# Last products of an encoder layer's MLP: row halves one after the other, the last product by output rows, and a shorter inverse root

## The chip, the cores and the metric

The kernel runs on one core of a Trainium2 chip. The metric is the device time of one execution in microseconds (us). The kernel before took 3382.24 us, the median of three runs (3379.86 to 3386.33).

## The reference

One layer of an encoder on 2048 rows of 1024 numbers, all in fp32, and a last RMSNorm:

```python
u = _rms_norm(h, norm_mix_g[l])
proj = u @ w_in[l]
hy = _short_conv_centred(proj[..., :HY_COLS], hy_conv_w[l], hy_conv_b[l])
spec = _hyena_filter_spectrum(L, hy_filt_w1[l], ...)
y_hy = _group_rms_norm(_hyena(hy, spec, hy_skip[l]), hy_norm_g[l], HYENA_GROUPS)
...
y_ml = _group_rms_norm(_mlstm_bidirectional(...), ml_norm_g[l], MLSTM_HEADS)
mixed = jnp.concatenate([y_hy, y_ml], axis=-1)
h = h + mixed @ w_out[l]
h = h + _cross_attention(_rms_norm(h, norm_x_g[l]), _rms_norm(mem, norm_mem_g[l]), ...)
h = h + jnp.square(jax.nn.relu(_rms_norm(h, norm_ff_g[l]) @ ff_w1[l])) @ ff_w2[l]
return _rms_norm(h, final_norm_g)
```

`_rms_norm(x, g)` is `x * rsqrt(mean(x*x) + EPS) * g` over a row. The change touches the last product (`@ ff_w2`), the residual sum behind it, the last RMSNorm, and the inverse root of every norm.

## The kernel before, in words

**Stages.** Row norms, the input projection, the filters and the FFT convolution, the mLSTM, the output projection, cross-attention, and the MLP follow each other. Every fp32 operand of a large product is split into a high and a low half in a rounded format (`halves`, `split`): ACT casts the high half, and DVE or GpSimd (POOL) subtracts to get the low half. One product is then three matmuls (`mm3`, L294 to L297: high by high, low by high, high by low) that add up in one PSUM bank.

**The MLP.** Both of its products use a Strassen-Winograd scheme of seven products instead of eight. The last one, "down", runs over four quarters `o` of the inner dimension (4096), each with the seven products `i` in the order `ORDER_DOWN` = 1, 6, 7, 5, 3, 2, 4: 28 products `prods`, numbered n = 0 to 27. Each is done for two halves of the rows, `tp` = 0 and 1, and each such (n, tp) has four inner blocks k. So `down` lists 224 steps s = (n, tp, k); a step issues twelve matmuls of 128x512 (four output blocks m of 128, three matmuls each), a group (n, tp) 48. A group has four PSUM banks, of tag "mm" for half 0 and "hy" for half 1 (four buffers each). In the last block o = 3 (n = 21 to 27) the finished sums leave.

**Around a step.** `fetch_b(s + 3)` loads a block of activations `wr` from the scratch `hc` (DMA on SP's queue) and makes its halves `bh`, `bl` (six buffers each); from s = 200 on the subtraction is POOL's for k > 0. `fetch_a` makes the next product's weight halves `ah`, `al` (four buffers). Behind the last inner block four evictions add the banks into `acc[i, tp]` (L1576, DVE); the sums between the accumulators (`add`, L1542) run on DVE or POOL.

**The way out.** `acc` holds columns by rows; the output wants rows by columns. The list `outs` holds closures that are taken one or two at a time behind the steps' matmuls. `turn` (L1509 to L1512) makes four transposes of 128x128 on TensorE into a PSUM bank of the tag that the running group doesn't use, squares the bank on ACT with a sum per row into `ss` (L1511), and multiplies by the gain `gl` on DVE into another accumulator's space (L1512). `finish(c, ...)` (L1517 to L1533), for c = 0 to 3, 512 rows each, combines the two sums of squares with `rbp`, the earlier norm's 1/(mean square + EPS), takes the inverse root, scales eight tiles of 128x512 (ACT L1529, for the last row block DVE L1527 as well), and stores (L1533, SP's queue). Row blocks 1 and 3 finish earlier; block 0 finishes behind (27, 0) and block 2 behind (27, 1), the last group. The remaining turns and the finish of block 2 come after the loop (`for x in outs`).

**The inverse root.** `rsqrt` (L150 to L155) starts from a guess made on the number's bits, a shift and then a multiply and add, and does three Newton steps of three DVE instructions each. It is called 58 times, with names `xr`, `mr`, `hr`, `qr` and `or`.

**Order.** The instructions are ordered by a planner that estimates times (`schedule_with_timeline_sim=True`); the order in the text is only its starting point, except where `keep_in_program_order` pins an instruction. Pools with a fixed number of buffers set how far ahead it can go.

Of the kernel before, what the change touches and what calls it, by code (L numbers as in the profile page):

```python
# [19 lines left out]
D = 1024  # L20
# [77 lines left out]
class Prog:  # L98
# [45 lines left out]
    def rsqrt(self, pool, ms, name):  # L144
# [5 lines left out]
        nc.vector.tensor_scalar(yi, mi, 1, None, ALU.logical_shift_right)  # L150
        nc.vector.tensor_scalar(yi, yi, -1.0, float(0x5F3759DF), ALU.mult, ALU.add)
# [141 lines left out]
    def mm3(self, ps, lh, ll, rh, rl, start, stop):  # L293
        mm = self.nc.tensor.matmul  # L294
        mm(ps, lh, rh, start=start, stop=False)  # L295
        mm(ps, lh, rl, start=False, stop=False)  # L296
        mm(ps, ll, rh, start=False, stop=stop)  # L297
# [763 lines left out]
    def attention(self, es):  # L1061
# [66 lines left out]
        for c in range(4):  # L1128
# [134 lines left out]
            def stats(c=c, ssum=ssum):  # L1263
# [12 lines left out]
                nc.vector.reciprocal(rbp[:, 4 * c:4 * c + 4], rbp[:, 4 * c:4 * c + 4])  # L1276
# [12 lines left out]
    def halves(self, src, tags, bufs, eng):  # L1289
        hi, lo = (self.R.tile([128, 512], F32R, tag=n, name=n, bufs=bufs) for n in tags)  # L1290
        self.nc.scalar.copy(hi, src)  # L1291
        eng.tensor_tensor(lo, src, hi.bitcast(F32), ALU.subtract)  # L1292
        return hi, lo
# [72 lines left out]
    def ffn(self):  # L1366
# [7 lines left out]
        down = [(n, tp, k) for n in range(len(prods)) for tp in range(2) for k in range(4)]  # L1374
        aq, bq = {}, {}

        def fetch_a(n, k):
# [13 lines left out]
            aq[n, k] = self.halves(src, ("ah", "al"), 4, eng)  # L1391
# [90 lines left out]
        with tc.tile_pool(name="down", bufs=1) as B:  # L1482
# [21 lines left out]
            ss = B.tile([128, 4, 2, 4], F32, name="ss")  # L1504

            def turn(c, h, src, dst, t, tag):
# [5 lines left out]
                nc.vector.tensor_tensor(dst[:, t], pt, gl[:, 512 * h:512 * h + 512], ALU.mult)  # L1512

            def finish(c, dst, last):
                rb = self.rbp[:, 4 * c:4 * c + 4]
                m = B.tile([128, 4], F32, tag="mo", name="mo", bufs=2)
                nc.vector.tensor_tensor(m, ss[:, c, 0], ss[:, c, 1], ALU.add)  # L1517
                nc.vector.tensor_tensor(m, m, rb, ALU.mult)
                nc.vector.tensor_tensor(m, m, rb, ALU.mult)
                nc.vector.tensor_scalar(m, m, 1.0 / D, EPS, ALU.mult, ALU.add)  # L1520
                rv = self.rsqrt(B, m, "or")
                nc.vector.tensor_tensor(rv, rv, rb, ALU.mult)
                for h in range(2):
                    for t in range(4):
                        v = dst[h][:, t]
                        if last and t % 2:
                            nc.vector.tensor_scalar(v, v, rv[:, t:t + 1], None, ALU.mult)  # L1527
                        else:
                            nc.scalar.mul(v, v, rv[:, t:t + 1])  # L1529
                        if last and t % 2 or t == 3:  # L1530
                            n = 2 if last else 4
                            r0 = 512 * c + 128 * (t + 1 - n)
                            nc.sync.dma_start(  # L1533
                                out=self.out[r0:r0 + 128 * n, 512 * h:512 * h + 512].rearrange("(t p) c -> p t c", p=128),
                                in_=dst[h][:, t + 1 - n:t + 1])
# [3 lines left out]

            def add(i, j, tp, eng):  # L1540
                for m in range(4):
                    eng.tensor_tensor(acc[i, tp][:, m], acc[i, tp][:, m], acc[j, tp][:, m], ALU.add)  # L1542
# [3 lines left out]
            V, G = nc.vector, nc.gpsimd  # L1546
            for s, (n, tp, k) in enumerate(down):
# [3 lines left out]
                if s + 3 < len(down):  # L1551
                    fetch_b(s + 3, G if s > 199 and k else V)
# [6 lines left out]
                if k == 0:  # L1559
                    bank = [self.hy() if tp else self.mm() for _ in range(4)]  # L1560
                (ah, al), (bh, bl) = aq[n, k], bq.pop(s)
                for m in range(4):
                    msl = slice(128 * m, 128 * m + 128)
# [138 lines left out]
```

## Time and profile before

| | |
|---|---|
| median of three runs | 3382.24 us (3379.86 to 3386.33) |
| profiled execution, its own time | 3383.48 us |
| its span on the core | 3381.8 us |
| mean granted TensorE clock | 0.979 |
| TensorE busy (PE) | 3194.3 us, 94% |
| VectorE busy (DVE) | 2042.5 us, 60% |
| ScalarE busy (ACT) | 1492.4 us, 44% |
| GpSimd busy (POOL) | 1269.8 us, 38% |
| DMA | 674.55 MB, 199 GB/s over the span |

The durations come from the one profiled execution, and times in it count from the start of its span. A line of the timeline has start, duration, engine, line of the kernel, operation, and out<-in by the program's names; "xN" are N instructions taken together; what stands in brackets is the idle time of the engine just ahead and what ended it. A line of stretches gives the busy time of PE, PEld (weight loads), DVE, ACT and POOL, each with the number of instructions, then the granted clock, the DMA engines' share, and GB/s.

### The profile page before, as it was taken

Reading aid. Unit: us, or ns where it says so; the run is one execution under the profiler, and the core shown is the slowest. Engines: PE = TensorE matmul, PEld = TensorE weight load, DVE = VectorE, ACT = ScalarE, POOL = GpSimd, SP = SyncE. Lnnn points to the kernel's source line nnn. Section 1 sums busy time; section 2 is a strip of 40 time slices with the busy share of each in tenths; the row PEclk is TensorE's granted clock in tenths of the full one; section 3 lists DMA queues with packets and bytes.
Section 4 is the critical chain, followed back from the end, with each engine's and each line's share of the span. In section 5 each row is a group of like instructions: output and inputs, shape, how many; then the busy total and the mean of one; then the engine's idle time right before and its main releaser. Section 6 shows DMA issues by size and latency. Waiting matters only on the chain.

```text
span 3381.8 us, 46860 instructions
## 1 busy us (share of the span) xinstructions
PE 3194.3 (94%) x15671; PEld 2550.0 (75%) x15671; DVE 2042.5 (60%) x3711; ACT 1492.4 (44%) x2884; POOL 1269.8 (38%) x894
## 2 busy tenths in 40 slices
PE   6999999999898888799999999999999999999997
PEld 5646666677676788688887997788788887888876
DVE  7685225524546755777766554755855576555695
ACT  4344435523454235444444444555655543333335
POOL 2131001200222314544424012876766564434482
PEclk9999999999999999999999999999999999999998
DMA  5366889996998579857657444765654475444434
GB/s 165 117 208 206 286 282 256 271 325 238 241 240 279 172 229 273 275 154 231 184 162 253 147 132 161 224 205 179 207 167 158 147 244 171 128 140 135 133 94 159
DMA packets 480749, 674.55 MB, mean 199 GB/s; under 512 B 41738, under 2 KB 256848, under 8 KB 479484
## 3 DMA queue, kind: packets, MB, share of 16 engines
q1 hardware_dynamic: 478904, 668.70, 63.4%
q0 software_dynamic: 1600, 2.86, 0.4%
q8 instruction: 124, 2.03, 0.3%
q14 instruction: 117, 0.96, 0.1%
q10 hardware_dynamic: 4, 0.00, 0.0%
HBM read 452.23 MB, written 219.18 MB: 199 GB/s over the span
## 4 chain that ended last, share of the span: by engine, by line
PE 43%; DVE 7%; DMA 5%; issue 3%; POOL 2%; ACT 1%; SPq 1%; DVEq 0%; ACTq 0%; POOLq 0%
PE mm L295 9%; PE mm L297 9%; PE mm L296 9%; PE hy L297 5%; PE hy L295 4%; PE hy L296 4%; DVE wl L301 1%; DVE bl L1292 1%; POOL acc L1500 1%; DMA rw<-rows 1%; PE hy L1106 1%; DMA wr<-xs 1%; DMA wn<-in_x_dram 1%; DMA va<-vd 1%; DVE acc L1542 0%
## 5 line engine op out<-in xcount | busy, mean ns | idle before, releaser
L301 DVE TENSOR_TENSOR wl<-wn,wh 128x512 fp32r<-128x512 f32 (+1 forms) x352 | 274.6, 813 | 144.4 <-ACT wh L300 143.8
L1292 DVE TENSOR_TENSOR bl<-wr,bh 128x512 fp32r<-128x512 f32 x213 | 234.8, 1108 | 134.6 <-ACT bh L1291 132.2
L1291 ACT CAST ah<-w 128x512 fp32r<-128x512 f32 x284 | 176.2, 622 | 298.9 <-PE hy L296 152.7
L300 ACT CAST wh<-wn 128x512 fp32r<-128x512 f32 (+1 forms) x352 | 202.1, 617 | 216.2 <-PE mm L296 80.0
L295 PE MATMUL mm<-xh,wh 128*128 128x512 f32 x640 | 276.4, 432 | 8.7 <-ACT P L542 7.5
L739 POOL TENSOR_TENSOR b<-b,a 128x512 f32<-128x512 f32 x64 | 88.8, 1387 | 502.1 <-ACT b L737 201.1
L296 PE MATMUL mm<-xl,wh 128*128 128x512 f32 x640 | 266.4, 416 | 0.1
L297 PE MATMUL mm<-xh,wl 128*128 128x512 f32 x640 | 264.3, 413 | 0.3 <-DVE wl L301 0.3
L1292 DVE TENSOR_TENSOR al<-w,ah 128x512 fp32r<-128x512 f32 x236 | 226.9, 963 | 59.9 <-ACT ah L1291 59.7
L1291 ACT CAST bh<-wr 128x512 fp32r<-128x512 f32 x232 | 143.4, 621 | 244.3 <-PE mm L297 180.1
L297 PE MATMUL mm<-bh,al 128*128 128x512 f32 x576 | 224.4, 392 | 8.3 <-DVE al L1292 5.7
L295 PE MATMUL mm<-bh,ah 128*128 128x512 f32 x576 | 226.0, 392 | 0.0
L296 PE MATMUL mm<-bl,ah 128*128 128x512 f32 x576 | 225.0, 391 | 0.0
L295 PE MATMUL mm<-act,wh 128*128 128x512 f32 x512 | 201.4, 397 | 6.0 <-ACT wh L300 6.0
L296 PE MATMUL mm<-act,wh 128*128 128x512 f32 x512 | 203.0, 397 | 0.0
L297 PE MATMUL mm<-act,wl 128*128 128x512 f32 x512 | 201.1, 396 | 0.0
L1149 POOL TENSOR_TENSOR ssum<-ssum,sq 128x512 f32<-128x512 f32 x56 | 80.7, 1440 | 269.7 <-ACT sq L1148 268.2
L295 PE MATMUL hy<-bh,ah 128*128 128x512 f32 x448 | 175.2, 391 | 0.0
L296 PE MATMUL hy<-bl,ah 128*128 128x512 f32 x448 | 174.6, 390 | 0.0
L297 PE MATMUL hy<-bh,al 128*128 128x512 f32 x448 | 174.6, 390 | 0.0
L295 PEld LDWEIGHTS mm<-xh,wh 128*128 128x128 f32 x640 | 122.4, 191 | 56.7 <-issue 18.0
L295 PE MATMUL hy<-xh,ah 128*128 128x512 f32 x384 | 152.8, 398 | 7.6 <-ACT ah L1291 6.8
(379 smaller groups left out, 9021.1 us busy)
## 6 DMA issues: line engine op xcount, KB each, us to landing
wr<-hc SPq DMA_DIRECT2D x224, 256.0 KB
w<-in_ff_w_dram SPq DMA_DIRECT2D x176, 256.0 KB
a<-hd SPq DMA_DIRECT2D x128, 256.0 KB
hc<-t SPq DMA_DIRECT2D x128, 256.0 KB
wn<-in_w_in_dram SPq DMA_DIRECT2D x104, 256.0 KB
hc<-q SPq DMA_DIRECT2D x96, 256.0 KB
fs<-a SPq DMA_DIRECT2D x32, 512.0 KB
a<-fs SPq DMA_DIRECT2D x32, 512.0 KB
```

The lines of the kernel that those rows point to most:

```text
L295: mm(ps, lh, rh, start=start, stop=False)
L296: mm(ps, lh, rl, start=False, stop=False)
L297: mm(ps, ll, rh, start=False, stop=stop)
L300: self.nc.scalar.copy(hi, src)
L301: self.nc.vector.tensor_tensor(lo, src, hi.bitcast(F32), ALU.subtract)
L739: nc.gpsimd.tensor_tensor(xt, xt, hi[:, m], ALU.mult)
L1106: nc.tensor.transpose(pt[:, 128 * k:128 * k + 128], yn[:, 128 * k:128 * k + 128], self.ident)
L1149: nc.gpsimd.tensor_tensor(ssum, ssum, sq, ALU.add)
L1291: self.nc.scalar.copy(hi, src)
L1292: eng.tensor_tensor(lo, src, hi.bitcast(F32), ALU.subtract)
L1500: nc.gpsimd.tensor_tensor(v, v, ms[2 * tp + n], ALU.mult)
```

## The change

**Inverse root.** The shift is gone: the guess is one multiply and add with -0.5.

**The power of a row.** `rbp` now holds EPS times the square of (mean square + EPS) instead of its reciprocal, so that `finish` needs one instruction per part of the sum (`power`), then the root (`scale`), and no product behind it.

**Order of the steps.** `down` runs n = 0 to 25 as before, then half 0 of products 26 and 27, then half 1 of both. The weight halves of product 27, which both halves need, move to the ring `w` of 12 buffers.

**The last product.** For (27, 1) the loop index is the output block, and the four inner blocks are run through within it. Behind two of them the transposes of the previous block are issued (`turn_rows`: four transposes, four squares of 128x128, one gain multiply with the gain broadcast over the four tiles). These and the matmuls are pinned to the program's order. Behind the last matmul the last block is turned, and block 2 is finished.

**Stores.** The earlier ones go out on ACT's queue, 512 KB each; the last ones are 256 KB each, half of them on ACT's queue and half on SP's.

**Additions.** They are queued in `sums`, one per step and engine.

**Fetches.** Three blocks more are fetched at seven steps from the end, one at six, none at five; the other steps fetch `s + 3`, the first step of the last product too. The subtraction is POOL's from s = 204 on, unless the fetched step is a multiple of four.

```diff
-        nc.vector.tensor_scalar(yi, mi, 1, None, ALU.logical_shift_right)
-        nc.vector.tensor_scalar(yi, yi, -1.0, float(0x5F3759DF), ALU.mult, ALU.add)
+        nc.vector.tensor_scalar(yi, mi, -0.5, float(0x5F3759DF), ALU.mult, ALU.add)
...
-                nc.vector.reciprocal(rbp[:, 4 * c:4 * c + 4], rbp[:, 4 * c:4 * c + 4])
+                nc.vector.scalar_tensor_tensor(rbp[:, 4 * c:4 * c + 4], rbp[:, 4 * c:4 * c + 4], EPS,
+                                               rbp[:, 4 * c:4 * c + 4], ALU.mult, ALU.mult)
...
-        down = [(n, tp, k) for n in range(len(prods)) for tp in range(2) for k in range(4)]
+        down = [(n, tp, k) for n in range(26) for tp in range(2) for k in range(4)]
+        down += [(n, tp, k) for tp in range(2) for n in (26, 27) for k in range(4)]
...
+            def turn_rows(c, m, src, dst, tag):
+                pt = self.ps.tile([128, 512], F32, tag=tag, name=tag, bufs=4).rearrange("p (t c) -> p t c", t=4)
+                for t in range(4):
+                    tc.keep_in_program_order(
+                        nc.tensor.transpose(pt[:, t], src[:, m, 128 * t:128 * t + 128], self.ident))
+                for t in range(4):
+                    junk = B.tile([128, 512], F32, tag="junk", name="junk", bufs=1)[:, 0:128]
+                    tc.keep_in_program_order(
+                        nc.scalar.activation(junk, pt[:, t], AF.Square, accum_out=ss[:, c, 1 + m, t:t + 1]))
+                g = gl[:, 512 + 128 * m:640 + 128 * m].unsqueeze(1).broadcast_to([128, 4, 128])
+                tc.keep_in_program_order(V.tensor_tensor(dst[:, :, 128 * m:128 * m + 128], pt, g, ALU.mult))
+
+            def power(c, parts, hold=False):
...
+                for h in parts:
+                    d = V.scalar_tensor_tensor(m, ss[:, c, h], 1.0 / D, q, ALU.mult, ALU.add)
...
+            def store(c, dst, last):
+                rv = total[c]
+                for t in range(4):
+                    for h in range(2):
                         v = dst[h][:, t]
-                        if last and t % 2:
-                            nc.vector.tensor_scalar(v, v, rv[:, t:t + 1], None, ALU.mult)
+                        if last and (h or t % 2):
+                            V.tensor_scalar(v, v, rv[:, t:t + 1], None, ALU.mult)
                         else:
                             nc.scalar.mul(v, v, rv[:, t:t + 1])
...
+                        if last:
+                            r0 = 512 * c + 128 * t
+                            (nc.scalar if h == 0 else nc.sync).dma_start(
+                                out=self.out[r0:r0 + 128, 512 * h:512 * h + 512], in_=v)
+                        elif t % 2:
+                            r0 = 512 * c + 128 * t - 128
+                            nc.scalar.dma_start(
...
-                if s + 3 < len(down):
-                    fetch_b(s + 3, G if s > 199 and k else V)
+                end = len(down) - s
+                for f in {7: (3, 4, 5), 6: (5,), 5: ()}.get(end, (3,)):
+                    if s + f < len(down):
+                        fetch_b(s + f, G if s > 203 and (s + f) % 4 else V)
...
+                else:
+                    msl = slice(128 * k, 128 * k + 128)
+                    for j in range(4):
+                        (ah, al), (bh, bl) = aq[n, j], bq[s - k + j]
+                        self.mm3(bank[k], ah[:, msl], al[:, msl], bh, bl, j == 0, j == 3, True)
+                        if j == 1 and k:
+                            turn_rows(2, k - 1, acc[4, 1], acc[5, 1], "mm")
+                    v = acc[4, 1][:, k]
+                    if k == 3:
+                        power(2, (0, 1, 2), True)
+                    tc.keep_in_program_order(V.tensor_tensor(v, bank[k], v, ALU.add))
+                for eng, q in sums.items():
+                    if q:
+                        eng.tensor_tensor(*(q[0][0], *q.pop(0), ALU.add))
...
-            for x in outs:
-                x("mm")
+            assert not outs and not any(sums.values())
+            turn_rows(2, 3, acc[4, 1], acc[5, 1], "mm")
+            power(2, (3, 4))
+            scale(2)
+            store(2, (acc[7, 1], acc[5, 1]), True)
```

More of the change, by code (lines that the diff above doesn't have):

```diff
@@ L291, in column, with mm3 @@
         return t
[L293 to L297, printed above, removed]
+    def mm3(self, ps, lh, ll, rh, rl, start, stop, pin=False):
+        parts = ((lh, rh), (lh, rl), (ll, rh))
+        for n, (x, y) in enumerate(parts):
+            d = self.nc.tensor.matmul(ps, x, y, start=start and n == 0, stop=stop and n == 2)
+            if pin:
+                self.tc.keep_in_program_order(d)
     def split(self, hi, lo, src):
@@ L1511, in turn @@
                 nc.scalar.activation(junk, pt, AF.Square, accum_out=ss[:, c, h, t:t + 1])
[L1512 to L1524, printed above, removed]
+                V.tensor_tensor(dst[:, t], pt, gl[:, 512 * h:512 * h + 512], ALU.mult)
@@ L1528, in finish @@
                         else:
                             nc.scalar.mul(v, v, rv[:, t:t + 1])
[L1530 to L1535, printed above, removed]
+                        if last:
[5 more added lines that the diff above has]
+                            nc.scalar.dma_start(
+                                out=self.out[r0:r0 + 256, 512 * h:512 * h + 512].rearrange("(t p) c -> p t c", p=128),
+                                in_=dst[h][:, t - 1:t + 1])
```

58 lines of the change are left out of this document (39 added, 19 removed).

## The prediction

> **What bounds the kernel now.** I read the page first (busy shares, slices, chain), then busy time by stretches, then the last 75 us instruction by instruction.
>
> ```profile
> PE 3194.3 (94%) x15671; PEld 2550.0 (75%) x15671; DVE 2042.5 (60%) x3711; ACT 1492.4 (44%) x2884; POOL 1269.8 (38%) x894
> PE   6999999999898888799999999999999999999997
> PE 43%; DVE 7%; DMA 5%; issue 3%; POOL 2%; ACT 1%; SPq 1%; DVEq 0%; ACTq 0%; POOLq 0%
> 3220.00:3290.00 70.00, 65.93 (x294) 53.57 (x293) 70.00 (x67) 22.10 (x40) 62.50 (x39) 1.00 0.31 91
> 3300.00:3358.50 58.50, 58.50 (x299) 48.24 (x296) 38.92 (x76) 35.12 (x79) 22.51 (x18) 1.00 0.46 152
> 3358.50:3381.80 23.30, 2.46 (x21) 1.98 (x19) 9.60 (x43) 10.89 (x22) 0.00 (x0) 0.60 0.49 180
> ```
>
> The first column of times after each stretch's length is PE, then PEld, DVE, ACT, POOL. TensorE is busy 94% of the span and leads the chain. The reader is to see the change of regime at 3358.5: up to there PE is at 58.50 of 58.50 us, so each instruction added to it lengthens the span and nothing else does; behind it come 23.3 us in which PE is nearly idle and one chain of dependent steps runs. That tail is what this change goes at. Here it is:
>
> ```profile
> 3306.62 0.48 PE L295 MATMUL mm<-bh,ah 128*128 128x512 f32 x1
> 3319.92 0.48 PE L295 MATMUL hy<-bh,ah 128*128 128x512 f32 x1
> 3354.50 0.39 PE L295 MATMUL hy<-bh,ah 128*128 128x512 f32 x1
> 3354.73 0.39 PE L296 MATMUL hy<-bl,ah 128*128 128x512 f32 x1
> 3357.21 2.48 DVE L1576 TENSOR_TENSOR acc<-hy,acc 128x512 f32<-128x512 f32 x4
> 3358.16 0.39 PE L297 MATMUL hy<-bh,al 128*128 128x512 f32 x1
> 3358.39 1.91 PE L1509 MATMUL mm<-ident,acc 128*128 128x128 f32 x16
> 3360.55 0.66 PE L1509 MATMUL mm<-ident,acc 128*128 128x128 f32 x4 [0.25 <-DVE acc L1512]
> 3360.90 0.60 ACT L1511 ACTIVATE junk<-mm 128x512 f32<-128x512 f32 x1
> 3361.62 0.60 ACT L1511 ACTIVATE junk<-mm 128x512 f32<-128x512 f32 x1
> 3361.62 0.69 DVE L1512 TENSOR_TENSOR acc<-mm,gl 128x512 f32<-128x512 f32 x1
> 3366.43 0.16 DVE L155 SCALAR_TENSOR_TENSOR or_y<-or_t,or_y 128x4 f32<-128x4 f32 x1
> 3366.62 0.16 DVE L1522 TENSOR_TENSOR or_y<-or_y,rbp 128x4 f32<-128x4 f32 x1
> 3366.82 1.68 DVE L1527 TENSOR_SCALAR acc<-acc,or_y 128x512 f32<-128x512 f32 x4
> 3368.31 7.46 SPq L1533 DMA_DIRECT2D out_dram<-acc  x6
> ```
>
> The last matmul ends at 3358.16 + 0.39 = 3358.55. Four evictions, twenty transposes, squares and gain multiplies lead to the root's last step at 3366.62; then the rows are scaled and stored. Two row blocks of 512 rows (c = 0 and c = 2) finish there together, so 4.19 MB leave in the tail, as the DMA view of 3360 to 3382 (40 slices of 0.55 us) shows:
>
> ```profile
> GB/s 0 0 0 0 0 0 0 0 0 0 0 0 0 0 0 0 82 398 376 376 365 372 395 376 376 365 391 376 372 387 369 387 384 384 384 384 328 0 0 0
> DMA packets 2144, 4.19 MB, mean 191 GB/s; under 512 B 96, under 2 KB 96, under 8 KB 2144
> ```
>
> Bytes move from about 3369.2 to 3380.3 at some 379 GB/s: about 0.9 us after the first issue, and 1.5 us before the end. Tail: 3381.80 - 3358.55 = 23.25 us.
>
> **The tail, part by part.** (26,1) means product 26, row half 1. (a) Rows of half 0 now run (26,0), (27,0) before (26,1), (27,1), so c = 0 is scaled and stored under some 22 us of matmuls. This takes 2.1 MB out of the tail: 2.1 / 379 GB/s = 5.5 us; that cover is there unless c = 0's scalings came more than 15 us late. (b) The last product is made by output rows, and three of four blocks are evicted, transposed, squared and multiplied inside the passes of the next. What stays is one block:
>
> ```profile
> L1005 ACT ACTIVATE ht<-ht 128x128 f32<-128x128 f32 x64 | 19.0, 298 | 25.2 <-POOL ht L1002 25.2
> L1005 ACT ACTIVATION_READ_ACCUMULATOR ht<-ht 128x1 f32 x64 | 12.0, 187 | 0.0
> ```
>
> DVE finishing what it is in, up to 1.6 (between 0 and the 2.48 of four evictions; nearest is the two gain multiplies of 0.69 that stand ahead of it, 1.4, with their waits); eviction 2.48/4 = 0.62 with its hand-over 0.75; four transposes 0.5; four squares of 128x128 with their read-out at 0.298 + 0.187, partly overlapped, 1.7 (against 0.72 for one of 128x512, the pitch of 3360.90 and 3361.62); gain multiply 0.69; 11 small ops on 128x4 at the pitch 3366.62 - 3366.43 = 0.19, 2.2. Sum 7.5 to the root's last step, where before took 3366.62 + 0.16 - 3358.55 = 8.2. Then one scaling 1.68/4 = 0.42, 0.9 until data move, 5.5 for 2.1 MB, 1.5 behind: 8.3. New tail 15.8, against 23.25: **-7.4**. The stores come from two issuing queues at once; I give that nothing, since the 379 GB/s already hold while a single queue issues. The Trainium skill, "DMA: Bandwidth & Descriptors", section "Anatomy of one DMA", fits 2.0 us and bytes over 436 GB/s to a transfer: an estimate by it is 6.8 us where my rows give 0.9 + 5.5 + 1.5 = 7.9, so by the page the end would come 1.1 us earlier; the trace's rate lies below the page's, and the trace decides.
>
> **What the passes pay for it.** The matmul pitch is 3354.73 - 3354.50 = 0.23 us; a group of 48 with 20 transposes lasts 3319.92 - 3306.62 = 13.30, so a transpose costs (13.30 - 48 x 0.23)/20 = 0.11. Matmuls are the same in number. From (26,0) to the last matmul the transposes under passes were 20, 16, 16 and 16; by the order of the changed program they are 20, 32, none and 28, so 12 more: **+1.3**. (25,1) takes four more: **+0.45**. On a PE that is busy all the time these count in full.
>
> Waits that did not exist:
>
> ```profile
> 3278.65 0.50 PE L297 MATMUL mm<-bh,al 128*128 128x512 f32 x1 [2.35 <-POOL al L1292]
> 3279.07 3.47 DVE L1292 TENSOR_TENSOR bl<-wr,bh 128x512 fp32r<-128x512 f32 x2
> 3318.65 5.02 ACT L1529 ACTIVATE acc<-acc,or_y 128x512 f32<-128x512 f32 x8 [0.83 <-DVE or_y L1522]
> 3329.69 0.62 ACT L1291 CAST bh<-wr 128x512 fp32r<-128x512 f32 x1
> L217 ACTq DMA_DIRECT2D b<-in_hy_skip_dram x2: 209/357/505, 104.1 to 104.6; - x2
> ```
>
> (c) Since `fetch_b` gives POOL fewer halves, two or three subtractions of (25,1) move to DVE, where one costs 0.6 to 3.47/2 = 1.7; a gain multiply that frees a PSUM bank for (26,0) stands behind them. 0 to 1.7; I take the middle, **+1.1**. (d) At the first step of the last product the default fetch brings block 223 a second time, and the passes read this copy. Its cast (0.62) is queued on ACT behind c = 0's eight scalings (5.02) and four DMA issues (0.2 to 0.5 each by the only such row on ACT), and these wait for c = 0's root. Without the scalings it would be there early; with them all in the way PE waits 2.6. I take **+1.0**. (e) In the same product the eviction of an output block stands on DVE behind the previous block's gain multiply, which waits for the four squares on ACT behind that cast; the transposes, and with them PE, wait. Between 0, if ACT is free, and 2.65 (two multiplies 1.4, cast 0.62, rest of a square); taken near the middle, **+1.5**. (d) and (e) together reach 7.8 only if c = 0's root comes after all four evictions.
>
> **The rest of the kernel.** The inverse root loses one DVE op in 58 calls: 58 x 0.19 = 11.0 us if all lay on the path, 0 if none. PE is full in most slices, so I take **-0.5**. But a planner orders all instructions, and the order of PE differs, though only by a few places, in the filters, between some 855 and 1215 us and between 1325 and 1455 us.
>
> ```profile
> 862.48 2.08 PE L702 MATMUL hy<-b,em 128*128 128x512 f32 x2 [4.61 <-DVE b L740]
> 870.00:1215.00 345.00, 315.66 (x1564) 240.88 (x1563) 213.91 (x489) 150.62 (x257) 83.23 (x59) 0.97 0.79 226
> 1325.00:1455.00 130.00, 105.46 (x638) 91.22 (x637) 94.72 (x226) 61.30 (x187) 68.91 (x50) 0.93 0.83 262
> ```
>
> At 862.48 PE waited 4.61 us; in the new order eight transposes and 24 matmuls of the projection come first, yet those wait for a row block whose root runs on the same DVE, so I credit **-0.5**, and bound the reorder by one such wait each way, -4.6 to +4.6. The additions said to be spread stand on DVE and POOL in the same order as before up to the fourth last product: 0 there.
>
> **Sum.** -7.4 + 1.3 + 0.45 + 1.1 + 1.0 + 1.5 - 0.5 - 0.5 = -3.05. The profiled execution took 3383.48 (span 3381.8); it becomes about 3380.4. It lay 1.24 above the median of the runs, so on the median's scale 3382.24 - 3.05 = **3379.2**. The measurement can tell from no change about 0.2%, 6.8 us: my forecast is no measurable difference.
>
> **Rivals.**
>
> 1. The passes don't wait. If ACT's squares are never late, (c), (d) and (e) vanish, 3.6 us, and with another 1.5 from the start-up and the 862 us wait the gain is 8.1: 3374. For it: ACT is busy 35.12 of 58.50, so there is room. Against it: the order on ACT puts the scalings, issues and cast just there. Chance 0.30.
>
> 2. Slower, by the middle of the kernel. PE idles 345.00 - 315.66 = 29.3 and 130.00 - 105.46 = 24.5 us in the two reordered stretches, which shows that its order there is sensitive to what comes ready when. Should the new order add 10 us or more, the tail's gain is gone and the kernel is slower by over 0.2%: 10 of 53.8 is a fifth more idle time. With 13 us the time is 3392. For it: DMA shares of 0.79 and 0.83 and DVE two thirds busy there, so a block asked for late finds no slack. Against: shifts of a few places. Chance 0.12.
>
> 3. The clock. The trace shows a wait that halves TensorE's speed:
>
> ```profile
> 44.38 0.50 PE L295 MATMUL mm<-xh,wh 128*128 128x512 f32 x1 [2.78 <-ACT P L542]
> 45.64 0.63 PE L297 MATMUL mm<-xh,wl 128*128 128x512 f32 x1
> 48.20 0.63 PE L297 MATMUL mm<-xh,wl 128*128 128x512 f32 x1
> ```
>
> After 2.78 us of waiting, matmuls last 0.63 instead of 0.39 for 3.4 us or so, about 1.6 lost; the 2.35 us wait at 3278.65 lies in a stretch of granted clock 1.00. So if (d) and (e) fall into one wait above some 2.5 us, the last product loses 1.6 more: 3380.8. The Trainium skill, "TensorE: Matmul & The Clock Gate", Part 1, has the clock halved when the array has been idle and some 3.4 us of work until it is back, which by an estimate is 1.7 lost: the trace agrees with its 3.4. Chance 0.15, within my forecast's band.
>
> 4. The edits of the tail do nothing of what they say, because the long pole of the tail is (b) and not the stores: then tail -1.9 only and 3384.7. Against it: data move without a gap for 11 us. Chance 0.03.
>
> My forecast's case itself has 0.40. Cases one and two hold what leaves the band of 0.2%; of rival 1 a part stays inside, and of the forecast a part gains more: faster 0.31, same 0.57, slower 0.12. The range takes the reorder's 4.6 beyond rival 1's 3374 and reaches on the other side to two thirds of rival 2: 3369.5 to 3388.5.
>
> **What would show it.** Right: the last matmul 4 to 7 us later than 3358.55, the tail 15 to 17 us, out stores of c = 0 under matmuls, 2.1 MB after the last matmul at about 379 GB/s; waits of PE on transposes and on `bh` within the last product, 1 to 5 us in sum; the time of 3306.62's matmul within 5 us of before. Wrong: a tail above 18, waits above 8 in the last product, or a start of the last products moved by more than 5 us.

## The result and the profile after

| | median | lowest to highest | runs |
|---|---|---|---|
| before, beside it | 3381.05 us | 3378.57 to 3386.33 | 6 |
| after | 3397.73 us | 3388.10 to 3401.84 | 6 |

The ratio is 1.0039 (1.0020 to 1.0058): slower, by more than the 0.2% that I had called measurable, and above my range. A second set of nine runs gave 1.0042 (1.0027 to 1.0057). Executions of one kernel scatter by some 10 us either way, so spans of single traces are not compared below; stretches between the same two instructions are.

The page of the changed kernel, engines, slices of PE and chain:

```profile
PE 3199.7 (94%) x15671; PEld 2554.6 (75%) x15671; DVE 2031.8 (60%) x3648; ACT 1494.3 (44%) x2907; POOL 1264.6 (37%) x893
PE   7999999999999888799999999999999999999997
PE 45%; DVE 6%; DMA 5%; issue 3%; POOL 2%; ACT 1%; SPq 0%; POOLq 0%; DVEq 0%; ACTq 0%
```

Nothing on the page tells of a loss; TensorE is busy 5.4 us longer and stands in the chain for 45% of the span instead of 43%. The stretches at the end (columns as before) do:

```profile
3300.00:3370.50 70.50, 65.40 (x320) 51.79 (x318) 44.30 (x84) 46.61 (x118) 26.20 (x20) 0.98 0.45 153
3370.50:3386.40 15.90, 0.72 (x5) 0.42 (x4) 6.61 (x24) 3.15 (x12) 0.00 (x0) 0.60 0.36 132
```

Before, PE was busy in 58.50 of 58.50 us up to its last matmul; now it idles 5.1 of 70.5. The tail shrank to 15.9 from 23.3. The starts of the groups and the waits of TensorE (timeline of the changed kernel, PE):

```profile
3274.88 0.39 PE L295 MATMUL mm<-bh,ah 128*128 128x512 f32 x1
3293.51 0.50 PE L295 MATMUL hy<-bh,ah 128*128 128x512 f32 x1 [1.16 <-DVE acc L1518]
3308.46 0.48 PE L295 MATMUL mm<-bh,ah 128*128 128x512 f32 x1
3311.33 0.47 PE L295 MATMUL mm<-bh,ah 128*128 128x512 f32 x1 [0.91 <-DVE acc L1518]
3324.26 0.50 PE L295 MATMUL hy<-bh,w 128*128 128x512 f32 x1 [0.33 <-DVE acc L1518]
3339.78 0.47 PE L295 MATMUL mm<-bh,ah 128*128 128x512 f32 x1 [0.67 <-DVE acc L1518]
3350.78 0.39 PE L295 MATMUL hy<-bh,w 128*128 128x512 f32 x1
3356.64 0.50 PE L295 MATMUL hy<-bh,w 128*128 128x512 f32 x1 [1.36 <-ACT bh L1295]
3358.00 0.50 PE L295 MATMUL hy<-bl,w 128*128 128x512 f32 x1 [0.85 <-POOL bl L1296]
3359.52 0.66 PE L1524 MATMUL mm<-ident,acc 128*128 128x128 f32 x4 [0.79 <-DVE acc L1613]
3360.38 0.63 PE L295 MATMUL hy<-bl,w 128*128 128x512 f32 x1
3361.66 0.63 PE L295 MATMUL hy<-bl,w 128*128 128x512 f32 x1
3370.17 0.40 PE L295 MATMUL hy<-bh,w 128*128 128x512 f32 x1
3372.69 0.66 PE L1524 MATMUL mm<-ident,acc 128*128 128x128 f32 x4 [2.12 <-DVE acc L1613]
```

The starts are those of (25,0), (25,1), (26,0), (27,0), (26,1), (27,1); before, (25,0) started at 3275.69, (25,1) at 3292.89, (26,0) at 3306.62. The last matmul ends at 3370.57, 12 us later than before, while (25,0) began 0.8 earlier. The stretch from the start of (25,0) to the end of the span is 3386.4 - 3274.88 = 111.5 us, against 106.1. So in this execution the whole loss, 5.4, is in the last products. But this was the fastest of its six executions. The second trace of the same kernel (e1) is already 5.9 us later than before at (25,0), and its stretch is 110.9. Where those 5.9 us come from, the experiments tell in part.

ACT, POOL and DVE at the head of (27,1), in the changed kernel:

```profile
3351.07 2.56 ACT L1554 ACTIVATE acc<-acc,or_y 128x512 f32<-128x512 f32 x4 [2.14 <-DVE or_y L154]
3354.15 1.93 ACT L1554 ACTIVATE acc<-acc,or_y 128x512 f32<-128x512 f32 x3
3355.99 0.60 ACT L1295 CAST bh<-wr 128x512 fp32r<-128x512 f32 x1
3356.67 1.28 POOL L1296 TENSOR_TENSOR bl<-wr,bh 128x512 fp32r<-128x512 f32 x1 [5.85 <-ACT bh L1295]
3358.77 0.69 DVE L1613 TENSOR_TENSOR acc<-hy,acc 128x512 f32<-128x512 f32 x1 [0.15 <-PE hy L295]
```

The cast of the second copy of block 223 stands on ACT behind block 0's scalings, which began when the root let them at 3351.07. POOL subtracts after it. The passes wait for both, the eviction follows, and the transposes wait for that.

The bytes after the last matmul (DMA view of 3364.4 to 3386.4, 40 slices):

```profile
GB/s 0 0 0 0 0 0 0 0 0 0 0 0 0 0 0 0 0 0 0 0 0 0 0 0 0 0 45 395 372 387 369 365 395 369 399 372 343 4 0 0
DMA packets 1152, 2.10 MB, mean 95 GB/s; under 512 B 128, under 2 KB 128, under 8 KB 1152
```

Half the bytes, the same rate.

### The profile page after: what moved, and what is told of

Same layout as the page of the kernel before. It is cut to its first block, busy times and chain, and to the rows that moved or that the text cites. A ratio compares the mean times of both kernels' runs of the same rounds, so it can differ in the third digit from the quotient of the medians.

```text
span 3386.4 us, 46842 instructions
## 1 busy us (share of the span) xinstructions
PE 3199.7 (94%) x15671; PEld 2554.6 (75%) x15671; DVE 2031.8 (60%) x3648; ACT 1494.3 (44%) x2907; POOL 1264.6 (37%) x893
## 4 chain that ended last, share of the span: by engine, by line
PE 45%; DVE 6%; DMA 5%; issue 3%; POOL 2%; ACT 1%; SPq 0%; POOLq 0%; DVEq 0%; ACTq 0%
PE mm L295 28%; PE hy L295 14%; DMA rw<-rows 1%; DVE wl L301 1%; DVE bl L1296 1%; PE hy L1106 1%; DMA wr<-xs 0%; PE hy L986 0%; DVE al L1296 0%; DMA wn<-in_x_dram 0%; DMA w<-in_ff_w_dram 0%; PE hy L988 0%; DMA wn<-in_w_out_dram 0%; PE hy L1214 0%; DVE acc L1616 0%
## 5 line engine op out<-in xcount | busy, mean ns | idle before, releaser
L295 PE MATMUL mm<-act,wh 128*128 128x512 f32 x1024 | 325.3, 397 | 7.8 <-ACT wh L300 7.8
L1296 DVE TENSOR_TENSOR bl<-wr,bh 128x512 fp32r<-128x512 f32 x215 | 247.7, 1159 | 125.7 <-ACT bh L1295 125.6
L295 PEld LDWEIGHTS mm<-act,wh 128*128 128x128 f32 x1024 | 192.5, 189 | 47.5 <-ACT wh L300 8.7
L295 PE MATMUL mm<-wh,act 128*128 128x256 f32 x1024 | 191.6, 287 | 4.1 <-ACT act L304 2.4
L295 PEld LDWEIGHTS mm<-wh,act 128*128 128x128 f32 x1024 | 162.5, 194 | 4.7 <-ACT act L304 2.6
L295 PE MATMUL hy<-bh,ah 128*128 128x512 f32 x416 | 162.4, 390 | 1.3 <-DVE acc L1518 1.2
L295 PE MATMUL hy<-bh,al 128*128 128x512 f32 x416 | 162.1, 390 | 0.0
```

Source lines behind the costliest of these rows:

```text
L295: d = self.nc.tensor.matmul(ps, x, y, start=start and n == 0, stop=stop and n == 2)
```

## The experiments

Measured beside the kernel before on the same chip, in five rounds each. Ratios are to the kernel before. The last column is the stretch from the start of (25,0) to the end of the span, in the run's trace (before: 106.1 us).

| run | ratio (95%) | (25,0) to end, us |
|---|---|---|
| e1 changed kernel again | 1.0042 (1.0027 to 1.0057) | 110.9 |
| e2 change, old root | 1.0021 (1.0005 to 1.0037) | 111.4 |
| e3 shorter root alone | 1.0016 (0.9997 to 1.0035) | 106.4 |
| e4 change, no second fetch | 1.0009 (0.9994 to 1.0024) | 108.8 |
| e5 as e4, old root | 0.9996 (0.9984 to 1.0008) | 107.1 |
| e6 as e5, POOL's share as before | 0.9997 (0.9983 to 1.0011) | 106.1 |
| e7 as e5, last product by inner blocks | 0.9987 (0.9975 to 0.9999) | 105.1 |
| e9 shorter root, row norms only | 0.9991 (0.9973 to 1.0009) | 106.1 |
| e10 shorter root, all others | 1.0045 (1.0027 to 1.0063) | 105.9 |
| e11 e7 with e6's edit | 0.9995 (0.9980 to 1.0010) | 104.8 |
| e12 e11, shorter root in row and last norms | 0.9990 (0.9975 to 1.0004) | 103.8 |
| e13 e11, earlier stores on SP | 0.9983 (0.9967 to 0.9999) | 103.7 |
| e14 shorter root, mLSTM norm only | 1.0027 (1.0017 to 1.0038) | 108.0 |
| e15 shorter root, Hyena norm only | 1.0022 (1.0011 to 1.0034) | 106.1 |
| e16 shorter root, ahead of cross-attention only | 1.0008 (0.9997 to 1.0019) | 106.6 |
| e17 change, shorter root in row and last norms only | 1.0021 (1.0006 to 1.0036) | 109.6 |
| e18 e13 with the roots of e12 | 1.0006 (0.9991 to 1.0022) | 103.3 |
| e19 e7 with the earlier stores on SP | 1.0006 (0.9991 to 1.0021) | 104.5 |

Seven of these kernels (before, e3, e9, e10, e14, e15 and e16) have the last products as they were, and their last column runs from 105.9 to 108.0. So a difference of up to 2 us in this column is not settled by one trace on each side.

**Two places or one.**

> The changed kernel once more, to see how its executions scatter and to get a second trace. Where it stands so far: the profiled execution was 4.6 us longer in span than before, of which the trace puts -0.8 ahead of the last ninety us and +5.4 in them, while four of six executions lay another 8 to 14 us higher. Theory A (two places): the +5.4 of the last products is in every execution, and the rest comes from the middle, where the shorter root has changed the order, so executions scatter between 3388 and 3402. Theory B (one place): the last products cost 5 us or 15 us from execution to execution, the middle nothing. Both expect 3388 to 3402; a trace of a long execution would show by the same instruction's start at the head of the last column block whether it is already late there (A) or not (B).

e2, on the changed kernel:

```diff
-        nc.vector.tensor_scalar(yi, mi, -0.5, float(0x5F3759DF), ALU.mult, ALU.add)
+        nc.vector.tensor_scalar(yi, mi, 1, None, ALU.logical_shift_right)
+        nc.vector.tensor_scalar(yi, yi, -1.0, float(0x5F3759DF), ALU.mult, ALU.add)
```

> The changed kernel with the old inverse root (shift, then multiply and add); all else of the change stays. Its order of TensorE's instructions is that of the kernel before up to the last column block. Theory A: the scatter goes, all executions lie about 5 us over before (3384 to 3391). Theory B: median 10 to 17 us over before, scattered as the changed kernel.

e3 is the reverse edit on the kernel before.

> The kernel before with the shorter inverse root alone. Its order of TensorE's instructions is that of the changed kernel up to the last column block. Theory A: median 5 to 12 us over before, scattered from -2 to +14. Theory B: within 2 us of before.

e2 measured +0.21% and e3 +0.16%; together about the 0.42% of the changed kernel. That fits two places, as theory A has it, though e3's interval reaches down to no change; e10 and e14 below show the second place clear of noise. Theory A's other half fell: the scatter did not go with the root (e2 lay between 3381 and 3401). Scatter belongs to every kernel here, the one before included (3374.56 to 3398.85 in 33 runs).

**The second fetch.** e4, on the changed kernel:

```diff
-                for f in {7: (3, 4, 5), 6: (5,), 5: ()}.get(end, (3,)):
+                for f in {7: (3, 4, 5), 6: (5,), 5: (), 4: ()}.get(end, (3,)):
```

> The changed kernel without the second fetch of block 223 at the first step of the last product, so that its passes read the first copy. Both theories: the wait of 1.4 us for its cast and of 0.85 us for its subtraction goes, and with it perhaps the half clock that follows (3.4 us at half speed, 1.7 us): 2 to 4 us less than the changed kernel on the same scatter. A rival: the transposes of row block 0 then wait as long for the eviction, and it gains under 1 us.

> The changed kernel with the old inverse root and without the second fetch of block 223. Theory A, by now in three parts: the tail's new waits, of which the second fetch is some 3.7 us in the last product; the middle's new order; both add up. It expects the last product at 15 to 16 us instead of 19.6, and the time 1 to 4 us over before. Rival (the last product waits for its evictions whatever the fetch does): 18 us or more, and 5 us over before.

In e4's trace (27,1) starts at 3353.02; the waits left in it, and its end:

```profile
3353.02 0.39 PE L295 MATMUL hy<-bh,w 128*128 128x512 f32 x1
3363.16 0.66 PE L1524 MATMUL mm<-ident,acc 128*128 128x128 f32 x4 [1.29 <-DVE acc L1613]
3363.57 0.48 PE L295 MATMUL hy<-bh,w 128*128 128x512 f32 x1
3363.89 0.39 PE L295 MATMUL hy<-bl,w 128*128 128x512 f32 x1
3368.59 0.40 PE L295 MATMUL hy<-bh,w 128*128 128x512 f32 x1
```

(27,1) lasts 3368.99 - 3353.02 = 16.0 us instead of 3370.57 - 3350.78 = 19.8, and its matmuls keep their full pace: 3.8 us for one loop entry that fetched a block already there. e5's group lasts as long, 16.2, a little over the theory's 15 to 16. The whole stretch gained 2.1 to 2.7 us from the changed kernel's two traces to e4, and 4.3 from e2 to e5. In the times, e4 lies 0.33% under e1 and e5 0.25% under e2, which is more than the traces show; the intervals are wide enough to cover it. e5 came out level with before, not 1 to 4 us over it.

**Subtractions, output rows, stores.** e6, on e5:

```diff
-                        fetch_b(s + f, G if s > 203 and (s + f) % 4 else V)
+                        fetch_b(s + f, G if s > 199 and k else V)
```

> The same as the run of e5, and besides POOL's share of the low halves as before (from step 200 on, for k > 0). Theory A: the groups (25,0) and (25,1) were 1.4 and 1.2 us longer in the changed kernel because DVE had two more subtractions each beside POOL's additions; they return to 17.2 and 14.2 (0.45 more than before for four transposes), and the time is 2 us under that of e5. Rival (the lock only moves: POOL's longer queue makes the low halves late): the groups stay as long or the matmuls wait for bl, and the time is that of e5 or more.

(25,0) and (25,1) returned to 17.2 and 14.2 us, from 18.6 and 14.9 in e5. (26,0) grew from 15.3 to 17.2, and the stretch gained 1.0 instead of 2: half of the theory, half of the rival. The times of e5 and e6 do not differ (0.9996 and 0.9997).

e7 takes the last product out of its special case (`for f in (3,)`, and the twelve matmuls of a step in the old loop for all steps), and the last block's turns come behind it:

```diff
...
-            turn_rows(2, 3, acc[4, 1], acc[5, 1], "mm")
-            power(2, (3, 4))
+            for f in outs:
+                f("mm")
+            power(2, (0, 1))
             scale(2)
             store(2, (acc[7, 1], acc[5, 1]), True)
```

> The same as the run of e5, but the last product by inner blocks as before: four evictions, 16 transposes and four squares of 128x512 follow the last matmul, the row halves still one after the other, so that the row block 0 is stored under the last products. Theory: the last product lasts about 12.9 us (11.0 and 16 transposes) instead of 15 to 16, and the tail is 17.5 to 19 instead of 15.8 us, which gives the same time as e5 within 1 us: the division by output rows brings nothing that its waits don't take. Rival: the tail is 21 us, and the time 3 us above that of e5.

The end of e7's matmuls, and its stores (timelines of PE and of SP's queue):

```profile
3366.91 0.39 PE L296 MATMUL hy<-bh,w 128*128 128x512 f32 x1
3367.14 2.08 PE L1516 MATMUL mm<-ident,acc 128*128 128x128 f32 x16
```

```profile
3375.36 3.09 SPq L1558 DMA_DIRECT2D out_dram<-acc  x4
```

The span is 3383.7, so the tail is 3383.7 - 3367.30 = 16.4 us, with four evictions, 16 transposes and squares of 128x512 behind the last matmul. In e5, its pair with the division by output rows, it is 16.3, and over all runs with the division 15.8 to 16.4. So the division brought next to nothing, where the theory had given it 2 to 3 us. Its passes hold twelve transposes more and the waits for evictions: (27,1) lasts 16.2 us in e5 and 12.9 in e7, and the stretch with the division is 2 us longer (107.1 against 105.1). e7 is the only one of these that came out a little below before.

> The run of e7 (row halves one after the other, last product by inner blocks, no second fetch, old root), with POOL's share of the low halves as before. Theory: the time from the start of (25,0) to the end was 106.1 us in before, 111 in the changed kernel, 107.1, 106.1 and 105.1 in the runs of e5, e6 and e7; both savings add up to 104, 2 us under before. Rival: 105 to 106, as e6's saving was partly a longer (26,0).

104.8: between theory and rival.

e13, on e11:

```diff
-                            nc.scalar.dma_start(
+                            nc.sync.dma_start(
                                 out=self.out[r0:r0 + 256, 512 * h:512 * h + 512].rearrange("(t p) c -> p t c", p=128),
```

> The run of e11 with the earlier out stores (512 KB each) on SP's queue instead of ACT's. The issues cost ACT 0.4 us each, four for a row block, ahead of casts and squares. Theory: the groups (26,0) and (27,0) shorten by 0.5 to 1.5 us, the time by as much. Rival: on SP the stores stand ahead of the loads of wr and wait for the scalings, which makes the last blocks late: 1 to 4 us more.

The stretch fell to 103.7, as the theory has it. SP did not hold up the loads: ACT's casts waited 14.2 us in sum for blocks `wr` of `hc` from 3265 to 3375 us, where in e11 it was 21.3. e19, e7 with the same edit, gave 104.5, so 0.6 and 1.1 us for ACT's freed queue in two pairs, both within what single traces differ by. e19's time, expected 0 to 0.1% under before, came out 0.06% over it.

> The run of e7 with the earlier stores on SP's queue, so with the change's share of POOL. Theory: the groups (25,0) and (25,1) are 19 and 15 us long, as in e7, and the sum from (25,0) to the end is 104 to 105; the time 0 to 0.1% under before. Rival: it is as e13, and the share of POOL costs nothing.

**The root's calls.** In e9, e10 and e14 to e16 the shorter root is behind a condition on the call's name, in the kernel before:

```diff
+        if name == "xr":            # e9; e10: name != "xr"; e14: "mr"; e15: "hr"; e16: "qr"
+            nc.vector.tensor_scalar(yi, mi, -0.5, float(0x5F3759DF), ALU.mult, ALU.add)
+        else:
             nc.vector.tensor_scalar(yi, mi, 1, None, ALU.logical_shift_right)
...
```

> The kernel before with the shorter root only in the norms of 128-row blocks ahead of the projections (26 of the 58 calls). Its order of TensorE's instructions is that of the shorter root around 850 to 900 us, and that of before from about 1230 to 1320 us. In the four traces with the shorter root everywhere TensorE gains 4 to 8 us about 860 to 890 us, and loses 10 to 16 us in three places from 1386 to 1561 us. Theory: the two come from different calls, so this kernel keeps the gain and has not the loss: 3 to 8 us under before. Rival: the gain is given back at the next wait on a transfer, whatever the order later: within 2 us of before.

> The kernel before with the shorter root in all calls but those of the row norms ahead of the projections (32 of the 58). Theory: the losses seen in the four traces with the shorter root everywhere (4 to 5 us about 1386 to 1412 us, 3 to 4 about 1481 to 1490, 2 to 5 about 1552 to 1561) belong to these calls, so they are in this trace too, without the gain at 862 us: 3 to 10 us over before. Rival: the losses come from the head start that the gain brings (transfers that are not yet there), and this kernel has neither: within 2 us of before.

> The kernel before with the shorter root only in the norm of the mLSTM's heads (16 calls). Theory M (these calls carry the loss, as the order moves between about 1258 and 1305 us, ahead of the losses at 1386 to 1561 us): 0.3 to 0.5% over before, with the losses in the trace. Theory H (the Hyena's calls): within 0.1%.

> The kernel before with the shorter root only in the norm of the Hyena's groups (8 calls). Theory M: within 0.1% of before. Theory H (these calls carry it, as the order moves between about 975 and 1028 us and what is shifted there meets the mLSTM's transfers later): 0.3 to 0.5% over before.

> The kernel before with the shorter root only in the four calls ahead of cross-attention. Both theories: within 0.1% of before; a third, that the eleven matmuls it moves about 1358 us delay the loads behind them, has the loss here: 0.3% or more.

e10 shows it without any edit of the last products: 32 instructions fewer, +0.45%, more than the 3 to 10 us expected. e14, the mLSTM's calls alone, is at +0.27%, a little under theory M's 0.3 to 0.5%. For the place I took the stretch from the 6050th to the 7200th of TensorE's records, in the mLSTM's part with its norms. One stretch of each kernel, in the order before, after, e14, e15, e17:

```profile
1377.70:1578.70 201.00, 181.86 (x1152) 161.50 (x1151) 149.69 (x363) 96.90 (x271) 82.30 (x59) 0.97 0.67 207
```

```profile
1368.90:1582.30 213.40, 187.06 (x1152) 165.05 (x1151) 147.66 (x355) 96.75 (x271) 81.52 (x59) 0.93 0.65 196
```

```profile
1372.40:1585.70 213.30, 190.06 (x1152) 167.30 (x1151) 146.93 (x356) 96.57 (x272) 80.99 (x59) 0.91 0.64 197
```

```profile
1381.00:1585.00 204.00, 183.01 (x1153) 162.82 (x1152) 149.99 (x363) 96.67 (x271) 83.56 (x60) 0.96 0.68 205
```

```profile
1364.90:1570.70 205.80, 183.88 (x1153) 163.53 (x1152) 148.20 (x363) 96.28 (x272) 82.94 (x60) 0.96 0.66 203
```

The work is the same but for two matmuls (1152 in all). With the shorter root in the mLSTM's norm the stretch is 213 us, without it 201 to 206. This holds in all twenty traces: 213.3 to 215.6 in the six with it (mean 214.4), 200.4 to 206.6 in the fourteen without (mean 203.6), and the two sets do not overlap. In the six, the order has changed by a few places around the 6050th record. Between records at which the orders agree, the 5850th and the 7200th, the difference of the means is 10.2 us (246.4 to 249.0 against 234.1 to 240.2). Up to the 8500th, some 225 us later, it is 7.1 (469.0 to 471.6 against 460.1 to 465.9): 3 us come back, and about 7 are lost.

From the 6050th to the 7200th record DVE has 2.0 us less to do in the changed kernel and 2.8 in e14 than before. TensorE waits more, and at a lower granted clock: 0.91 to 0.93 in the six, 0.94 to 0.97 in the others. Of the 10.8 us between the two means, 6.5 are idle time of TensorE and 4.3 longer busy time of as many matmuls. What TensorE waited for in it, before and in e14 (waits):

```profile
PE hy L1106 <- DMA wn<-yh: 7.6, 2, 7.3
PE mm L296 <- DVE wl L301: 4.3, 4, 2.1
PE mm L297 <- DVE act L305: 1.7, 2, 1.1
```

```profile
PE hy L1109 <- DMA wn<-yh: 7.8, 2, 6.8
PE mm L298 <- ACT wh L303: 6.2, 4, 2.4
PE hy L1109 <- DVE mr_t L157: 2.6, 1, 2.6
PE mm L298 <- ACT act L307: 1.9, 1, 1.9
```

The long wait for the transfer `yh` is in both. The waits for ACT's casts `wh` and `act` and for the root's own step look new, but e17, which has no loss here, shows two of the three as well:

```profile
PE hy L1110 <- DVE mr_t L156: 2.4, 1, 2.4
PE mm L299 <- ACT act L308: 2.3, 1, 2.3
PE mm L299 <- ACT wh L304: 0.4, 1, 0.4
```

What goes with the loss is the wait of the products into `mm` for the cast `wh`: 2.9 to 6.2 us in the six traces with the loss, at most 1.0 in the fourteen others. So the order that the planner chose for fewer instructions is a worse one on this chip. TensorE's own order narrows the place down: e14's differs from before in several places, and only two of them are in no kernel without the loss, from the 5864th to the 6131st record (1346 to 1399 us in before) and six records at the 7083rd. Which instruction there is at fault, on TensorE or on another engine, is not separated.

The row norms were to do the opposite. From the 3300th to the 3500th record (about 835 to 900 us) the eight traces with the shorter root in the row norms take 59.3 us in the mean (55.2 to 63.0), the twelve without 63.0 (60.3 to 65.3). But the order differs there too: 12 of TensorE's first 3500 records are others in the eight. From the 3300th to the 4230th, where the orders agree again, it is 249.0 (240.9 to 257.5) against 251.0 (246.4 to 260.0). So a gain of the row norms is not shown; e9's time, 0.09% under before, does not clear its interval either.

e15 measured 1.0022, clear of its interval, without the loss in the mLSTM stretch. Both theories had one culprit, and there are two. The Hyena's loss lies at its own norm: from the 4250th to the 4460th record (about 1090 to 1145 us), at which all orders agree, e15 and e10 take 57.3 us, the eighteen others 51.7 to 54.5. TensorE waits there for steps of the roots (e15, waits), where the two longest waits of the kernel before are 5.8 and 2.5 us:

```profile
PE mm L423 <- DVE xr_t L157: 7.5, 1, 7.5
PE hy L756 <- DVE hr_t L156: 4.3, 1, 4.3
```

That is some 4 of e15's 7 us; the rest stays open. In the four traces with the shorter root in the row norms as well as in the Hyena's (the changed kernel's two, e3 and e4) the same stretch takes 52.1 to 52.9 us: this loss is no part of the change. So the calls' costs do not add up one by one. e9, e14, e15 and e16 sum to +0.48%, and e3, with all calls at once, measured +0.16% (-0.03 to 0.35).

e16 (1.0008) is within what can be told from none.

**The parts together.**

> The whole change, with the old root in the mLSTM's and the Hyena's norms and ahead of cross-attention. If parts add up: 0.15 to 0.2% over before by the last products, less 0.1% or so that the row norms gain: 0.05 to 0.15% over before, no loss at 1386 to 1561 us in the trace, and the time from the start of (25,0) to the end 111 us as in the changed kernel. Rival (the parts don't add up, the whole has a cost of its own): 0.3% or more.

e17 measured 1.0021, as e2 did and above the 0.05 to 0.15% expected, and its stretch in the mLSTM is 205.8. With the calls of the mLSTM left alone their loss is gone from the trace, and the last products' is left (109.6 against 106.1); the row norms took nothing off that the time would show.

> The run of e11 with the shorter root in the row norms ahead of the projections and in the last norm. Theory: the parts add up: 2 us of the tail and some 3 us (0.1%) of the row norms, so 3377 to 3383 where before has 3386, the first version clear below before. Rival: the row norms' gain is one lucky execution, and this is 2 us under before.

> The run of e13 (halves one after the other, last product by inner blocks, POOL's share and the queue of the earlier stores as before) with the shorter root in the row norms and the last norm. Theory: from the start of (25,0) to the end 103 to 104 us, 2 to 2.5 less than before, and TensorE 3 to 4 us less about 862 to 890 us: 0.15 to 0.25% under before. Rival: the parts don't add up and it is within 0.1%.

e12 and e18 have some of the shortest stretches at the end, 103.8 and 103.3, but 0.9990 and 1.0006 in time, so e18's time goes to its rival. No version is clear below the kernel before; e13 (0.9983) and e7 (0.9987) have intervals that end at 0.9999, and among eighteen runs one or two such can be chance: e18 and e19, built on them, came out at 1.0006. What is 2 to 3 us in a trace is not settled by twelve executions that scatter by 10.

## Why the prediction was wrong

I forecast -3.05 us and no measurable difference; by the ratio it is +13 (0.39% of 3381, 7 to 20 by its interval), outside my range. Two steps failed, by about 8 us each. Either alone would have left the time within the range.

- **The rest of the kernel: the first step that failed.** I counted the root at -0.5 and the new order at -0.5, bounded by 4.6 either way. In the traces the mLSTM's norms cost +7, and a gain elsewhere is not shown. The bound was one wait at one place, 862 us, where I had looked; the reordering between 1325 and 1455 us I had priced only as rival 2. That rival is what happened: its first and largest step, 5 us, lies at 1386 to 1412 us, and two more follow at about 1481 to 1490 and 1552 to 1561 us, behind the stretch that it names. Together they have the price that I gave it, 10 us or more, of which 3 come back later. Rival 2 alone would have ended near 3387 with these 7 us; the waits below made up the rest. I put its chance at 0.12 because TensorE's order differs by a few places only; a few places were enough.
- **The tail, -7.4: right, for a reason half wrong.** It is 15.8 us long, as worked out: 7.2 to the root's last step (forecast 7.5, before 8.2) and 8.6 behind it (forecast 8.3). But I gave the division by output rows the first part, and e7 without it has 7.5 there and 16.4 in all, beside 16.3 in e5 with it: the earlier stores of block 0 did nearly all.
- **Transposes, +1.3 and +0.45: right.** (26,1), which has none, lasts 3350.78 - 3339.78 = 11.0 us.
- **Waits, +1.1, +1.0 and +1.5: the second step that failed, 11.2 against 3.6.** (c) was to be the wait for a bank of (26,0), at +1.1 (the middle of its 0 to 1.7 would have been 0.85). In its place (25,0) and (25,1) cost 1.4 and 1.2 - 0.45 = 0.8, since two subtractions had moved in (25,0) too: with POOL's old share, in e6, both lengths return. (26,0) is 15.8 instead of 13.3, +2.5. TensorE idles 1.4 us of that, mostly for gain multiplies on DVE that free a bank (0.91, 0.33), and ACT meanwhile waits 4.2 us for a weight block of product 27; the rest stays open. (27,0) is 15.5, where 32 transposes make 14.6: +0.9, for which I had nothing. (27,1) is 19.8 instead of 14.2: +5.6, where (d) and (e) had 2.5. The second fetch was seen, with its right chain, and taken at 1.0 of at most 2.6; with what it set off (POOL's subtraction, the late eviction, the clock) it cost 3.8 in (27,1).
- **The clock, rival 3: it came, not by its condition.** No wait in (27,1) reached 2.5 us; three of 1.36, 0.85 and 0.79 within 4 us were followed by matmuls of 0.63 for some 3 us. And in (25,0) of the changed kernel one wait of 2.35 us was followed by half speed, so the 2.5 us that I read out of two waits are no bound (rows in the last section). By the Trainium skill, "TensorE: Matmul & The Clock Gate", Part 1, the clock is set by how busy the array has been recently: the trace agrees with that, at 3.0 us of waits in a stretch from 3355.3 to 3359.5.

From the last products the sum is +5.4 instead of -2.05 (4.8 in the second trace), from the rest +7 instead of -1: +12.4, near the 13 measured, whose interval is wide enough for other small parts.

## What to carry to other kernels

Where a planner orders the whole program, an edit in a helper that is called everywhere is not priced by its instructions. Measure it alone, and call by call: one instruction fewer cost about 7 us in the mLSTM's norms and 4 in the Hyena's, these only as long as the row norms kept the old root. When orders differ, compare times only between instructions at which they agree again; a stretch that ended inside the reordered part gave the row norms a gain of 3.7 us, which cannot be told from scatter where the orders agree again. Before a stage's end is split finer, try the coarse step alone: moving one row block's stores ahead gave the tail's 7 us, while the split of the last product shortened it by about 0.1 and left the whole 2 us longer. An entry in a prefetch table that falls to a default is worth reading twice: one needless load, cast and subtraction cost 3.8 us in the last product, because they stood in the queue of the engines that the last passes wait for.

## What the runs showed of the hardware

Whether a wait halves the granted clock depends on when it falls, and not on its length alone. In the clock records of all twenty traces it changes only at marks 3.41 us apart. The wait of 2.35 us for the low half `al` in (25,0) is in the kernel before (its row stands in the prediction) and in the changed one:

```profile
3277.84 0.55 PE L295 MATMUL mm<-bh,al 128*128 128x512 f32 x1 [2.35 <-POOL al L1296]
3278.18 0.63 PE L295 MATMUL mm<-bh,ah 128*128 128x512 f32 x1
```

Two stretches between such marks, in the kernel before and then in the changed one:

```profile
3274.63:3278.04 3.41, 1.67 (x8) 1.05 (x6) 3.41 (x3) 0.00 (x0) 3.41 (x3) 1.00 0.25 76
3278.04:3281.46 3.42, 2.81 (x12) 2.17 (x12) 3.42 (x3) 1.14 (x2) 3.42 (x3) 1.00 0.00 1
```

```profile
3274.75:3278.16 3.41, 1.06 (x5) 0.58 (x4) 3.41 (x3) 0.38 (x1) 3.41 (x3) 1.00 0.33 77
3278.16:3281.57 3.41, 3.41 (x9) 2.67 (x8) 3.41 (x3) 0.76 (x2) 3.41 (x3) 0.50 0.10 21
```

Before, a mark cuts the wait in two, TensorE is busy for 1.67 of the 3.41 us, and the next stretch has the full clock. In the changed kernel the wait falls into one stretch, TensorE is busy for 1.06 us of it, and the next stretch has half the clock. Over the twenty traces the stretch with this wait was followed by half speed where TensorE had been busy for 0.28 to 0.42 of it (thirteen traces), and by full speed at 0.45 to 0.58 (seven). The busy share is not the whole rule: in (27,1) the three short waits left it at 0.52, and half speed followed.

Half speed did not lengthen (25,0): the group lasts 18.67 us in e19 at a granted clock of 1.00 and 18.63 in the changed kernel at 0.91, and 17.22 in e15 at 0.90 and 17.20 before at 1.00. Before, DVE is busy in all of its 17.2 us, so TensorE does not set the pace there.

In the mLSTM stretch the lower clock comes on top of the waits: a mean of 0.93 over 213.4 us is some 30 us at half speed, where before has 0.97 over 201.0, some 12. Half of the difference, 9 us, is the most that the clock can have added; a part of it falls into the waits themselves. TensorE's busy time there rose by 5.3 us, from 181.86 to 187.06. So where TensorE sets the pace, more waiting can be paid for a second time, in matmuls at half speed.
